# Rows after the experts by plain loads and summed in PSUM, two strict orders, and linear attention's heads by turns

## The chip, the cores and the metric

The kernel runs on one core of a Trainium2 chip. The metric is the device time of one execution in microseconds (us); the times of several runs are given as their median. The engines: PE (TensorE, matrix products) with its weight loads (PEld), DVE (VectorE), ACT (ScalarE), POOL (GpSimd) and SP (SyncE, here a queue that issues transfers). ACT and POOL issue transfers too. Products end in PSUM, everything else is in SBUF or in device memory (DRAM). PE's clock has two levels, 1.2 and 2.4 GHz; the profile gives the granted clock as a share of the higher one.

## The reference

A transformer block of two layers over 512 latent and 256 context rows of 1024 columns, then a second block of another kind over the 512 latent rows. Per layer of the first block, in the reference's words:

```python
h_lat = layer_norm(ALPHA * h_lat + mods[:, :, 2] * o_lat, ln_g[i, 0], ln_b[i, 0])   # after the mixer
f_lat = modulate(h_lat, mods[:, :, 3], mods[:, :, 4])
y_lat = moe(f_lat)                                       # each row goes to two of 32 experts
h_lat = layer_norm(ALPHA * h_lat + mods[:, :, 5] * y_lat, ln_g[i, 1], ln_b[i, 1])
```

Layer 0 does the same for the context rows, and layer 1's mixer begins by modulating the result. The second block begins with a root-mean-square norm, and one of its three branches is a gated linear attention in chunks, four heads with keys of 64 and values of 128.

## The kernel before

The rows live in `self.res`, six blocks of 128 rows by 1024 columns. Each expert scatters its weighted product rows to a DRAM buffer `y_d` by indirect transfers on POOL's queue (`store`, L1632 ff.): the first choices of all rows in its first half, the second choices in its second. Rows that overflow an expert's two halves of 64 go through up to a few extra tiles (`extra`), each of them behind a branch; in this data layer 0 has two extra tiles, of which the second fills both halves, and layer 1 has none.

Two places read `y_d` back. The first is the start of layer 1's mixer (`mixer_cd`), six blocks; the second the start of the second block (`second_body`), four. At both, `products` (L1729) loads the first half on ACT's queue into a buffer and accumulates the second half straight into `self.res` by a transfer of POOL's queue; then an addition on DVE (or, for two blocks at the second place, POOL) makes the sum with the residual, and a layer norm follows: statistics by `bn_stats` in two halves, an inverse root by a chain of one-column DVE operations, and a scale and shift on ACT (`normed`, first place) or on DVE (second place).

First place: each block is then turned by eight PE transposes and modulated (`modulate`), half by ACT, half by DVE; the result is split into a high and a low part (ACT rounds, POOL subtracts, L465) and projected by `project_window`, whose `finish` turns queries and keys one block later. Weights stream through four raw buffers on SP's queue (`Stream`) and are split into high and low parts in the same way, by ACT (L247) and DVE (L248). On POOL, `gain` and `bias` of the norm are applied to the first four blocks of `self.res` (L1069, L1070), whose result is needed only after the attention.

Second place: `front` adds, norms, writes the rows to DRAM, and norms them again; `back` turns and splits them and projects V. `piped(4, front, back, 2)` runs `front` two blocks ahead.

At both places the framework's planner orders the instructions of each engine, from its own costs. Under `tc.manual_schedule(engines=...)` the named engines keep the order in which the code is written; the experts' loop already does that for PE, ACT and DVE.

Linear attention (`gla`): for two pairs of heads and eight levels, each head's four blocks of 128 rows make products of 64 rows by 128 columns (L2091), into a PSUM tile per head; a masked copy on DVE (L2092) takes each tile into `ST`. The two heads of a pair lie in rows 0 to 63 and 64 to 127. The other branch's convolution projections fill in between.

Of the kernel before, what the change touches and what calls it, by code (L numbers as in the profile page):

```python
# [13 lines left out]
F32 = mybir.dt.float32  # L14
# [9 lines left out]
P = 128  # L24
# [159 lines left out]
class Kern:  # L184
# [262 lines left out]
    def modulate(self, x, b, layer, aT, places, ps):  # L447
# [3 lines left out]
        for k0 in (0, 4):  # L451
# [13 lines left out]
            (nc.gpsimd if layer else nc.vector).tensor_sub(aT[1][:, k0:k0 + 4, tok], v, aT[0][:, k0:k0 + 4, tok])  # L465
# [338 lines left out]
    def mixer_cd(self, atp, then):  # L804
# [3 lines left out]
        with ExitStack() as es:  # L808
# [15 lines left out]
            ys, at = [t[:, i * D:(i + 1) * D] for i in range(2)], [t[:, i * 512:(i + 1) * 512] for i in (4, 5, 6)]  # L824
            t = qp.tile([P, 3584], F32, tag="QK", name="t_qk")
            ys, gain = ys + [t[:, i * D:(i + 1) * D] for i in range(2)], t[:, 2 * D:3 * D]
            ys += [qp.tile([P, D], F32, tag=x, name="ys") for x in ("VW", "KX")]
            bias = qp.tile([P, D], F32, tag="VW", name="bias")
# [3 lines left out]
            for b in range(NB):  # L832
                self.products(0, b, ys[b])
# [5 lines left out]
            st = Stream(self, sp, plan, 4, 5, 768)  # L839
            nc.sync.dma_start(gain, self.bcast_rows(A["ln_g"][0, 1], D))  # L840
            nc.sync.dma_start(bias, self.bcast_rows(A["ln_b"][0, 1], D))
# [7 lines left out]
            nc.vector.tensor_scalar_mul(nsink, sink, -1.0)  # L849
# [200 lines left out]
            pc = ps.tile([P, 2, 2, KC], F32, tag="aux", name="pc")  # L1050
            for i in range(2):
                self.transpose(pc[:, i].rearrange("p w k -> p (w k)"), shsc[i])
            nc.scalar.activation(self.mcol[:, 1].rearrange("p i k w -> p i w k"), pc, AF.Copy)
# [1378 lines left out]
```

## Time and profile before

| | |
|---|---|
| time, median of 3 runs | 3341.03 us (3340.9 to 3345.55) |
| profiled execution's own time | 3345.23 us |
| its span | 3343.4 us, mean granted clock 0.958 |
| PE busy | 3016.8 us, 90% |
| DVE busy | 1502.2 us, 45% |
| ACT busy | 1015.6 us, 30% |
| POOL busy | 608.1 us, 18% |
| DMA | 647 MB, mean 194 GB/s |

The span is from the first to the last instruction of the profiled execution; its own time is 1.8 us longer. A matrix product of fp32 operands shows as two records. Busy shares are averages over stages with different limits, so stages are read one by one below.

### The profile page before, as it was taken

How to read it: one execution, taken by the hardware profiler on the slowest of the kernel's cores; microseconds unless marked ns; L12 is line 12 of the kernel's file. 1: busy time of each engine (PE TensorE's matmuls, PEld its weight loads, DVE VectorE, ACT ScalarE, POOL GpSimd, SP SyncE). 2: the span in 40 equal slices, each digit the busy share in tenths (PEclk: the TensorE clock that was granted, in tenths of full speed). 3: DMA queues.
4: the chain of work that ended last, by engine and by line, in shares of the span. 5: the costliest groups of instructions: out<-in, count | busy, mean ns of one | idle time of the engine just before them, and what ended most of it. 6: DMA issues, size and time to landing. Idle time of an engine off the chain costs nothing. (4 is left out here: it accounts for less than half of the span.)

```text
span 3343.4 us, 50272 instructions
## 1 busy us (share of the span) xinstructions
PE 3016.8 (90%) x19017; PEld 2180.2 (65%) x19017; DVE 1502.2 (45%) x3382; ACT 1015.6 (30%) x2180; POOL 608.1 (18%) x572
## 2 busy tenths in 40 slices
PE   7999999799999938998799998579999999979998
PEld 4677757555555527887555544258788777758887
DVE  3578866443222247765521212254544443364533
ACT  2445561111111015764111111123343433233321
POOL 1101012243422233011221211110221400010000
PEclk9999999799999968999799999889899999989999
DMA  7433152999999741113697999822121222322232
GB/s 268 157 98 106 58 170 105 356 393 418 393 419 418 313 143 37 51 42 109 242 386 283 411 418 403 322 97 75 58 79 64 76 73 91 139 78 99 101 120 76
DMA packets 142672, 647.34 MB, mean 194 GB/s; under 512 B 27458, under 2 KB 35170, under 8 KB 81074
## 3 DMA queue, kind: packets, MB, share of 16 engines
q1 hardware_dynamic: 117346, 598.03, 46.3%
q0 software_dynamic: 22192, 36.24, 3.5%
q10 hardware_dynamic: 2848, 9.19, 0.8%
q8 instruction: 187, 3.06, 0.4%
q14 instruction: 99, 0.81, 0.1%
HBM read 670.18 MB, written 35.03 MB: 211 GB/s over the span
## 5 line engine op out<-in xcount | busy, mean ns | idle before, releaser
L1600 PE MATMUL u<-raw,xs 128*64 128x256 f32 x5312 | 596.6, 382 | 19.6 <-DMA raw<-in_k_w 19.3
L1600 PEld LDWEIGHTS u<-raw,xs 128*64 128x64 f32 x5312 | 378.3, 137 | 219.0 <-DMA raw<-in_k_w 23.1
L248 DVE TENSOR_TENSOR wl<-raw,wh 128x2048 fp32r<-128x2048 f32 (+3 forms) x146 | 257.3, 1768 | 392.3 <-ACT wh L247 391.5
L241 PE MATMUL pm<-hTh,wh 128*128 128x512 f32 x872 | 343.7, 394 | 1.7 <-DVE hTl L248 1.4
L243 PE MATMUL pm<-hTh,wl 128*128 128x512 f32 x872 | 341.3, 392 | 1.1 <-DVE wl L248 1.1
L242 PE MATMUL pm<-hTl,wh 128*128 128x512 f32 x872 | 341.7, 392 | 0.0
L247 ACT ACTIVATE wh<-raw 128x2048 fp32r<-128x2048 f32 (+3 forms) x148 | 219.3, 1487 | 390.9 <-PE pm L242 178.0
L1620 PE MATMUL y<-raw,gs 128*64 128x512 f32 x1328 | 300.4, 597 | 4.3 <-ACT gs L1615 1.5
L1605 DVE TENSOR_TENSOR sg<-sg,u 128x256 f32<-128x256 f32 x132 | 55.4, 421 | 513.5 <-PEq L1653 299.8
L243 PE MATMUL pm<-wh,aTl 128*128 128x384 f32 (+2 forms) x576 | 200.8, 349 | 8.4 <-POOL aTl L465 8.4
L241 PE MATMUL pm<-wh,aTh 128*128 128x384 f32 (+2 forms) x576 | 203.3, 354 | 3.7 <-ACT wh L247 2.0
L242 PE MATMUL pm<-wl,aTh 128*128 128x384 f32 (+2 forms) x576 | 199.1, 346 | 0.6 <-DVE wl L248 0.6
L1620 PEld LDWEIGHTS y<-raw,gs 128*64 128x64 f32 x1328 | 89.0, 136 | 169.6 <-issue 155.7
L1604 ACT ACTIVATE sg<-u 128x256 f32<-128x256 f32 x132 | 50.8, 385 | 481.6 <-PE u L1600 315.9
L1626 DVE SCALAR_TENSOR_TENSOR ys<-y,rt_sw,gate 128x512 f32<-128x512 f32 x128 | 93.5, 748 | 226.3 <-PE y L1620 226.3
L241 PEld LDWEIGHTS pm<-hTh,wh 128*128 128x128 f32 x872 | 163.6, 188 | 37.6 <-DVE hTl L248 1.8
L243 PEld LDWEIGHTS pm<-hTh,wl 128*128 128x128 f32 x872 | 163.5, 188 | 36.1 <-DVE wl L248 1.6
L242 PEld LDWEIGHTS pm<-hTl,wh 128*128 128x128 f32 x872 | 163.6, 188 | 34.3
L1615 ACT ACTIVATE gs<-t 128x512 f32<-128x512 f32 x66 | 39.5, 598 | 332.7 <-PE t L271 301.9
L1298 POOL DMA_INDIRECT xg<-f_d,rt_row x64 | 68.5, 1070 | 395.8 <-PE t L271 369.3
L271 PE MATMUL t<-ident,p 128*128 128x128 f32 x704 | 122.0, 284 | 6.7 <-ACT pT L888 1.0
L243 PEld LDWEIGHTS pm<-wh,aTl 128*128 128x128 f32 x576 | 114.4, 199 | 15.0 <-POOL aTl L465 10.0
(559 smaller groups left out, 5551.2 us busy)
## 6 DMA issues: line engine op xcount, KB each, us to landing
raw<-in_k_w SPq DMA_DIRECT2D x408, 1024.0 KB
raw<-in_k_sb SPq DMA_DIRECT2D x79, 1024.0 KB
raw<-in_mod_w SPq DMA_DIRECT2D x160, 256.0 KB
raw<-in_k_ab SPq DMA_DIRECT2D x24, 384.0 KB
raw<-in_k_cd SPq DMA_DIRECT2D x24, 384.0 KB
raw<-in_k_mod SPq DMA_DIRECT2D x8, 1024.0 KB
raw<-in_k_w_out SPq DMA_DIRECT2D x8, 1024.0 KB
raw<-in_k_sb SPq DMA_DIRECT2D x12, 512.0 KB
```

The costliest lines, as they stand in the source:

```text
L241: nc.tensor.matmul(out, lh, rh, start=start, stop=False)
L242: nc.tensor.matmul(out, lh, rl, start=False, stop=False)
L243: nc.tensor.matmul(out, ll, rh, start=False, stop=stop)
L247: self.nc.scalar.activation(h, x, AF.Copy)
L248: (sub or self.nc.vector).tensor_sub(l, x, h)
L271: self.nc.tensor.transpose(out, in_, self.ident[:k, :k])
L1298: self.nc.gpsimd.indirect_dma_start(out=x, out_offset=None, in_=self.f_d[:nb * P], in_offset=bass.IndirectOffsetOnAxis(ap=gi, axis=0), bou ...
L1600: nc.tensor.matmul(pu[c][i][64 * n:64 * n + 64], xs[:, k, tok], w[:, k % 4, n * 256:(n + 1) * 256], start=k == 0, stop=k == KC - 1)
L1604: nc.scalar.activation(sg[c], pu[c][0], AF.Silu)
L1605: nc.vector.tensor_mul(sg[c], sg[c], pu[c][1])
L1620: nc.tensor.matmul(py[c][64 * n:64 * n + 64], gs[:, c, k % 2, k // 2], W[k // 2][:, k % 2, n * 512:(n + 1) * 512], start=k == 0, stop=k == 3)
L1626: nc.vector.scalar_tensor_tensor(y, py[c], sw[:, 0], gate[:, 0], op0=OP.mult, op1=OP.mult)
```

## The change

Four edits. (1) `products` loads both halves by plain transfers, the first on ACT's queue, the second on SP's; nothing is accumulated by a transfer. `summed` adds the residual and both loaded rows in PSUM, by products with the identity: three per half of 512 columns. The norms read PSUM. Blocks 0 and 1 are loaded ahead of the first weights, the others behind. (2) Both starts are written in one strict order for PE, ACT, DVE and POOL. At the second place `front` is now in two parts, one block ahead. At the first place gain and bias are loaded into buffers of the last block and applied after the ordered stretch, and the modulation's subtraction runs on DVE. (3) In an extra tile the second scatter runs only if the second half has rows. (4) In the linear attention the products of the two heads alternate.

```diff
@@ modulate
-            (nc.gpsimd if layer else nc.vector).tensor_sub(aT[1][:, k0:k0 + 4, tok], v, aT[0][:, k0:k0 + 4, tok])
+            nc.vector.tensor_sub(aT[1][:, k0:k0 + 4, tok], v, aT[0][:, k0:k0 + 4, tok])
@@ mixer_cd
-            for b in range(NB):
-                self.products(0, b, ys[b])
+            for b in range(2):
+                self.products(0, b, *ys[b])
+            st = Stream(self, sp, plan, 4, 5, 768)
+            for b in range(2, NB):
+                self.products(0, b, *ys[b])
...
-            Ws = [st.get() for _ in range(4)]
-            first = project_window(0, Ws)
-            for b in range(NB + 1):
-                if b < NB:
-                    x = self.res[:, b]
-                    nc.vector.tensor_add(x, x, ys[b])
-                    self.normed(self.small, x, x, 1e-5 / ALPHA ** 2)
-                if b:
-                    n = self.res[:, b - 1]
-                    self.modulate(n, b - 1, 1, aT, at, ps)
-                if b > 1:
-                    next(first)
-            next(first)
+            def front(b):
+                x = self.res[:, b]
+                self.normed(self.small, self.summed(x, ys[b], ps), x, 1e-5 / ALPHA ** 2)
+            with tc.manual_schedule(engines={E.PE, E.Activation, E.DVE, E.Pool}):
...
+                front(0)
+                Ws = [st.get(0) for _ in range(4)]
+                first = project_window(0, Ws)
+                for b in range(NB + 1):
+                    if 0 < b < NB - 1:
+                        front(b + 1)
+                    if b < NB:
+                        self.modulate(self.res[:, b], b, 1, aT, at, ps)
+                    if b == 0:
+                        front(1)
+                    else:
+                        next(first)
+            gain, bias = last_ys
+            nc.sync.dma_start(gain, self.bcast_rows(A["ln_g"][0, 1], D))
+            nc.sync.dma_start(bias, self.bcast_rows(A["ln_b"][0, 1], D))
@@ experts, extra tiles
-                        for c in range(2):
-                            store(scaled(c, sw[:, c]), si[:, c:c + 1])
+                        ys = [scaled(c, sw[:, c]) for c in range(2)]
+                        store(ys[0], si[:, 0:1])
+                        with tc.If(store_more):
+                            store(ys[1], si[:, 1:2])
@@ products
-        self.nc.scalar.dma_start(out, self.y_d[b * P:(b + 1) * P])
-        self.nc.gpsimd.dma_start(self.res[:, b], self.y_d[(n + b) * P:(n + b + 1) * P], accum_op=OP.add)
+        self.nc.scalar.dma_start(first, self.y_d[b * P:(b + 1) * P])
+        self.nc.sync.dma_start(second, self.y_d[(n + b) * P:(n + b + 1) * P])
+    def summed(self, x, ys, ps):
+        pm = ps.tile([P, 2, 512], F32, tag="s", name="sum")
+        for n in range(2):
+            for i, t in enumerate((x, *ys)):
+                self.nc.tensor.matmul(pm[:, n], self.ident, t[:, n * 512:(n + 1) * 512], start=i == 0, stop=i == 2)
+        return pm.rearrange("p a c -> p (a c)")
@@ second_body
                 for b in range(4):
-                    self.products(1, b, second[b])
+                    self.products(1, b, *ys[b])
+                    if b == 1:
+                        nc.gpsimd.dma_start(g, self.bcast_rows(A["pre_mix_g_2"], D))
+                        self.ws = ws = weights()
...
-                    (nc.gpsimd if b > 1 else nc.vector).tensor_add(x, x, second[b])
-                    mean, r = self.norm_scale(self.small, x, 1e-5 / ALPHA ** 2)
-                    nc.vector.scalar_tensor_tensor(x, x, mean, gb[:, 0], op0=OP.subtract, op1=OP.mult)
+                    y = self.summed(x, ys[b], ps)
+                    mean, r = self.norm_scale(self.small, y, 1e-5 / ALPHA ** 2)
+                    yield
+                    nc.vector.scalar_tensor_tensor(x, y, mean, gb[:, 0], op0=OP.subtract, op1=OP.mult)
                     nc.vector.scalar_tensor_tensor(x, x, r, gb[:, 1], op0=OP.mult, op1=OP.add)
                     nc.sync.dma_start(self.x_d[b * P:(b + 1) * P], x)
-                    return self.rms_apply(x, g, xp)
+                    yield self.rms_apply(x, g, xp)
...
-                for _ in piped(4, front, back, 2):
-                    pass
+                with tc.manual_schedule(engines={E.PE, E.Activation, E.DVE, E.Pool}):
+                    f = front(0)
+                    next(f)
+                    n = next(f)
+                    Ws = [ws.get(0) for _ in range(2)]
+                    for b in range(4):
+                        if b < 3:
+                            f = front(b + 1)
+                            next(f)
+                        back(b, n)
+                        if b < 3:
+                            n = next(f)
+                        values(b)
@@ gla
+                    pg = [ps.tile([P, 512], F32, tag="aux", name="pg") for _ in range(2)]
+                    for b in range(4):
+                        t = slice(b * P, (b + 1) * P)
+                        for hh in range(2):
+                            d = slice(hh * 64, (hh + 1) * 64)
+                            nc.tensor.matmul(pg[hh][:, t], ls[d, t], rs[d, t], start=True, stop=True)
                     for hh in range(2):
-                        d = slice(hh * 64, (hh + 1) * 64)
-                        pg = ps.tile([P, 512], F32, tag="aux", name="pg")
-                        for b in range(4):
-                            t = slice(b * P, (b + 1) * P)
-                            nc.tensor.matmul(pg[:, t], ls[d, t], rs[d, t], start=True, stop=True)
```

## Rows read from the trace of the kernel before

**Rows 1.** Stretches: busy PE, PEld, DVE, ACT, POOL (instructions), clock, DMA share, GB/s

```profile
1194.70:1236.40 41.70, 0.54 (x2) 0.36 (x3) 16.11 (x39) 4.48 (x6) 5.45 (x7) 0.50 0.90 255
...
1236.40:1300.50 64.10, 44.52 (x218) 38.76 (x218) 49.74 (x122) 30.26 (x72) 37.64 (x24) 0.79 0.13 42
...
1300.50:1350.00 49.50, 47.99 (x363) 41.85 (x362) 42.92 (x136) 31.62 (x102) 5.84 (x7) 0.97 0.10 30
...
2147.00:2194.70 47.70, 0.04 (x1) 0.07 (x2) 27.06 (x69) 6.12 (x6) 12.97 (x10) 0.53 0.70 214
...
2194.70:2227.80 33.10, 31.46 (x224) 29.46 (x224) 16.31 (x51) 11.87 (x18) 2.88 (x2) 0.90 0.18 62
...
2290.00:2390.00 100.00, 98.31 (x549) 78.84 (x548) 55.12 (x88) 26.02 (x38) 3.31 (x5) 1.00 0.18 64
```

**Rows 2.** Timeline after the first experts: start, length (us), engine, line, operation

```profile
1194.72 1.78 SPq L66 DMA_DIRECT2D raw<-in_k_cd  x4
...
1196.63 0.84 ACTq L1732 DMA_DIRECT2D t_o<-y_d  x2
...
1235.11 1.24 ACT L445 ACTIVATE res<-res,ln_m,rs_y 128x1024 f32<-128x1024 f32 x1 [25.75 <-DVE ln_m L444]
...
1236.40 1.97 PE L271 MATMUL pt<-ident,res 128*128 128x128 f32 x8 [35.54 <-ACT res L445]
```

**Rows 3.** DMA issues after the first experts: count, size, median us to landing

```profile
res<-y_d POOLq DMA_DIRECT2D x6, 512.0 KB, 30.4
```

**Rows 4.** Lines that copy V: count, ns min/median/max, first, last start

```profile
L914 ACT ACTIVATE V<-pm x12: 203/221/235, 1255.4 to 1361.0; 128x64 f32<-128x64 f32 x12
...
L1816 ACT ACTIVATE V<-pm x4: 574/598/598, 2204.7 to 2227.8; 128x512 f32<-128x512 f32 x4
```

**Rows 5.** Timeline of PE, dilated attention's fp32 score products

```profile
2520.77 1.02 PE L2230 MATMUL s<-qk 128*128 128x512 f32 x2
...
2521.63 0.61 PE L2232 MATMUL s<-qk 128*128 128x128 f32 x4
```

**Rows 6.** Timeline at the second place

```profile
2151.63 1.98 ACTq L1732 DMA_DIRECT2D y<-y_d  x4
...
2193.06 1.28 DVE L1749 SCALAR_TENSOR_TENSOR rm_n<-res,rs_y,g 128x1024 f32<-128x1024 f32 x1
...
2194.66 1.94 PE L271 MATMUL pt<-ident,rm_n 128*128 128x128 f32 x8 [48.37 <-DVE rs_t L262]
...
2258.77 2.29 DVE L248 TENSOR_TENSOR wl<-raw,wh 128x2048 fp32r<-128x2048 f32 x1 [3.27 <-ACT wh L247]
```

**Rows 7.** Timeline of PE while the clock rises

```profile
2200.95 0.40 PE L242 MATMUL pm<-wl,hTh 128*128 128x256 f32 x1
...
2201.31 0.28 PE L241 MATMUL pm<-wh,hTh 128*128 128x256 f32 x1
```

**Rows 8.** Timeline of DVE, first place: one-column operations, one modulation

```profile
1246.05 2.09 DVE L266 SCALAR_TENSOR_TENSOR rs_y<-rs_t,rs_y 128x1 f32<-128x1 f32 x1
...
1248.06 0.40 DVE L461 TENSOR_SCALAR t_o<-pt,mcol 128x128 f32<-128x128 f32 x1
...
1265.45 0.14 DVE L257 TENSOR_SCALAR rs_i<-ln_v 128x1 int32<-128x1 int32 x1
...
1267.23 0.16 DVE L444 SCALAR_TENSOR_TENSOR ln_m<-ln_mv,rs_y 128x1 f32<-128x1 f32 x1
```

**Rows 9.** The subtraction's line on either engine

```profile
L465 DVE TENSOR_TENSOR aTl<-at,aTh x12: 672/688/693, 35.2 to 94.6; 128x512 fp32r<-128x512 f32 x12
...
L465 POOL TENSOR_TENSOR aTl<-t_o,aTh x12: 1262/1277/1511, 1243.3 to 1295.2; 128x512 fp32r<-128x512 f32 x12
```

**Rows 10.** Timeline of PE, linear attention

```profile
2309.95 1.76 PE L2091 MATMUL pg<-Pl 64*128 64x128 f32 x16 [0.27 <-DVE ST L2092]
```

**Rows 11.** Timeline of PE, experts' products on alternate column halves

```profile
1149.75 6.46 PE L1600 MATMUL u<-raw,xs 128*64 128x256 f32 x58
```

**Rows 12.** Timeline of PE's weight loads while routing, clock low

```profile
608.05 1.35 PEld L1366 LDWEIGHTS pp<-tok,marks 128*128 128x128 f32 x6 [2.04 <-DVE marks L1362]
```

More of the change, by code (lines that the diff above doesn't have):

```diff
@@ L823, in mixer_cd @@
             t = op_.tile([P, 7 * NLAT], F32, tag="oT", name="t_o")
[L824 to L828, printed above, removed]
+            last_ys, at = [t[:, i * D:(i + 1) * D] for i in range(2)], [t[:, i * 512:(i + 1) * 512] for i in (4, 5, 6)]
+            qk = [qp.tile([P, 3584], F32, tag="QK", name=f"t_qk{i}") for i in range(2)]
+            qk = [[t[:, i * D:(i + 1) * D] for i in range(3)] for t in qk]
+            vw, kx = ([qp.tile([P, D], F32, tag=x, name="ys") for _ in range(2)] for x in ("VW", "KX"))
+            ys = [*qk[0], *vw, *kx, *qk[1], *last_ys]
+            ys = [ys[2 * b:2 * b + 2] for b in range(NB)]
             shsc = [ap.tile([16, P], F32, tag="v", name="shsc") for _ in range(2)]
@@ L1704, in extra @@
                     for i, (gi, sw, si) in zip(js, tables):
-                        more = nc.values_load(gi[64:65], engines=[E.PE], min_val=0, max_val=2000000) < nt
+                        more, store_more = (nc.values_load(gi[64:65], engines=[eng], min_val=0, max_val=2000000) < nt
+                                            for eng in (E.PE, E.Pool))
                         W = s.take(4)
@@ L1727, in experts, with products @@
             extra(0)
-    def products(self, layer, b, out):
+    def products(self, layer, b, first, second):
         n = 4 if layer else 6
-        self.nc.scalar.dma_start(out, self.y_d[b * P:(b + 1) * P])
-        self.nc.gpsimd.dma_start(self.res[:, b], self.y_d[(n + b) * P:(n + b + 1) * P], accum_op=OP.add)
+        self.nc.scalar.dma_start(first, self.y_d[b * P:(b + 1) * P])
[6 more added lines that the diff above has]
+        return pm.rearrange("p a c -> p (a c)")
     def rms_scale(self, x, pool):
@@ L1779, in proj, with second_body @@
             self.mm3(pm[:, c:c + n], self.hTh[:, k, tok], self.hTl[:, k, tok], w[0][:, k], w[1][:, k], k == 0, k == KC - 1)
-    def second_body(self):
+    def second_body(self, weights):
         nc, tc, A = self.nc, self.tc, self.A
-        ws, proj_T = self.ws, self.proj_T
+        proj_T = self.proj_T
         with ExitStack() as es:
@@ L1793, in second_body @@
                 g = xp.tile([P, D], F32, name="g", bufs=1)
-                nc.gpsimd.dma_start(g, self.bcast_rows(A["pre_mix_g_2"], D))
-                second = [xp.tile([P, D], F32, tag="y", name="y", bufs=4) for _ in range(4)]
+                ys = [[xp.tile([P, D], F32, tag=f"y{b}{i}", name="y", bufs=1) for i in range(2)] for b in range(4)]
                 for b in range(4):
-                    self.products(1, b, second[b])
+                    self.products(1, b, *ys[b])
+                    if b == 1:
+                        nc.gpsimd.dma_start(g, self.bcast_rows(A["pre_mix_g_2"], D))
+                        self.ws = ws = weights()
                 gb = self.res[:, 4:6]
```

22 lines of the change are left out of this document (10 added, 12 removed).

## The prediction

> **What bounds the kernel now.** I read the page first: TensorE (PE) is busy for 90% of the span, and the slices show three dips. Then the table by stretches [rows 1], which says what each dip is. Two of them lie where this change works. After the first experts PE does 0.5 us of work in 41.7 us at a DMA share of 0.90, and then runs at a mean granted clock of 0.79, busy 44.5 of 64.1 us, while VectorE (DVE) is the fuller engine for what it has to do (49.7). After the second experts PE does nothing for 47.7 us and then is busy 31.5 of 33.1. The linear attention (2290 to 2390) is the opposite: PE 98.3 of 100 at full clock, DVE 55. So in the first two places what ends last is a wait for rows of products, and in the third it is PE itself.
>
> The timeline at the first place [rows 2] shows the loads released at 1194.7, when the last scatter of the experts lands, and the first normalised block leaving ScalarE (ACT) at 1235.1; PE's 35.5 us of waiting ends there. Beside the loads run six accumulating transfers of 512 KB which take 30.4 us each from issue to landing [rows 3]. The checkpoint I use for both places is the line that copies V out of PSUM, once per block [rows 4]: at the first place block 0 comes at 1255.4 and block 5 at 1300.5 (9.0 per block), at the second 2204.7 to 2227.8 (7.7 per block).
>
> **What a sum in PSUM costs.** Six fp32 identity products of 512 columns per block: 36 at the first place and 24 at the second. The nearest row is the score product of the dilated attention, of the same shape [rows 5]: a product appears as two records, and the next one starts 0.86 us later at full clock. Six are 5.2 us a block; at the lower level twice that. Coming from a long idle PE stays at the lower level for 6.5 us (first transpose at 2194.66 [rows 6], products 0.40 us long until 2201, 0.28 after [rows 7]). So the first sum after the wait takes 6.5 us for the first 3.25 and 1.95 for the rest, 8.4. This is new work on PE; it removes one 1.2 us addition per block from DVE or GpSimd (POOL), the accumulating traffic, and the waits on it.
>
> **First place, step by step.** (a) The pair of rows for block 0 is now issued first on two queues, ACT's at 1196.6 as before [rows 2]; 1.05 MB at the 255 GB/s of this stretch [rows 1] is 4.1 us, with a little for the small loads ahead of it: landed about 1202. (b) Sum 8.4: 1210.4. (c) Statistics: the second half, 0.64 (half of a 1.28 pass [rows 6]), and the chain of one-column operations, 1.9 from shift to scale [rows 8] plus 0.4 for two before it: 2.9; the pass on ACT 1.24 [rows 2]: 1214.6. (d) Eight transposes at the low level, 1.97 [rows 2]: 1216.6. (e) In the written order the sum of block 1 stands behind these transposes, partly at the low level (7), and that of block 2 (5.3) behind it: PE is at 1229. DVE meanwhile does the four weight splits, block 0's rounding and block 1's statistics. Transposes of block 1, then the projection of block 0 (24 products of 384 columns; at the second place 48 of 256 take 5.9 us, see there, so by columns 0.18 each: 4.4, up to half more with the clock low): V of block 0 at about 1236, 19 us ahead of now.
>
> From there it loses. The cycle in the written order runs across engines: sum 5.4, statistics 2.9, pass 1.24, ACT's part of the modulation 2.1 (four modulations at about 0.38, and a rounding at half a pass), the subtraction 0.69 [rows 9], DVE's four modulations (0.40 each with a little overlap [rows 8]) 1.4, and only then is a PSUM buffer free for the last QK transposes (0.5), behind which the next sum stands: 14.2 us against 9.0 now. PE's own work in it is 12.0, DVE's about 10, so neither engine sets it but the order. Block 1 follows block 0 by 10.7 while the pipe fills, blocks 2 and 3 by 14.2 each, the context blocks, which have no rotation and a narrow projection, by 10.8 and 4: 54 us, so block 5 at 1290, 10.5 us ahead of 1300.5.
>
> (f) The subtraction goes from POOL to DVE, 1.28 to 0.69 each [rows 9]; PE waited for it, and the sum above holds the new price. (g) The eight multiplications and additions of gain and bias, POOL's 2.4 us each, move from this stage to the one after it, as they now wait for rows that the last sum frees. Today they stretch DVE's one-column operations from 0.15 to as much as 2.1 us [rows 8]. In the next stage DVE is busy 42.9 of 49.5 us and PE 48.0 [rows 1]: little is hidden there. The bounds are 0 and 8 times 2; I take 5, nearer the low end, as many operations there read PSUM, and a PSUM read among the stretched ones keeps its 0.40 [rows 8]. (h) SP's queue takes six row loads it didn't have, with the first weights after the second; behind them stand the zero rows and the masks. At 255 GB/s all twelve row loads and the weights (7.9 MB) are in by about 1226, the masks soon after; the first attention scores need them after 1290: 0. POOL's queue loses its six loads, and nothing on it waits for more. First place: 5.5 us gained. Bounds: 16 gained, 5 lost.
>
> **Second place.** Pair issued at 2151.6 [rows 6], 1.05 MB at 214 GB/s [rows 1]: 2157. Sum 8.4: 2165.4. Statistics 2.8, two passes 2.5, a squaring pass on ACT 1.3, the chain 1.9, the pass with the gain 1.28: rows ready at 2175 (2194.3 now). Transposes: 2177. But the written order puts the two weight splits (2.29 each [rows 6]) and block 1's statistics (3.4) ahead of block 0's rounding on DVE: its products start at 2184.3. The first block took 8 us from its start while the clock rose, so V of block 0 at 2192, 12 us ahead of now. Then each block costs products 5.9 (7.7 now [rows 4], less 1.0 for transposes and 0.8 of short waits), the next sum 5.4 behind them, its statistics 2.8 and a rounding 0.66: 14.7 instead of 7.7. Today the additions and norms of later blocks lie ahead, on DVE and POOL, while PE waits. Two cycles of 14.7 and a last step of 9.3, which has no sum: 2231, 3 us later than 2227.8. In each cycle PE idles some 2.6 us at a stretch, and at the first place a busy share of 0.7 went with a clock of 0.79 [rows 1]; I add 1 us per cycle. Second place: 6 us lost. Bounds: 3 gained (the pair lands 3 earlier, order as good as now), 16 lost. The weight loads move behind two pairs of rows; they have until 2171 and land by then at this rate.
>
> **The linear attention.** 128 products (64 rows by 128 columns) take their heads in turn. Now 16 records, 8 products, take 1.76 us from first start to last end [rows 10]: 0.1 us a record, 26 us in all, on an engine without slack. If neighbours of different row halves run at once, half goes: 13. One row speaks for it: the experts' products, which use alternate column halves, take 6.46 us for 58 records of 256 columns, 0.11 each [rows 11], where half of the 0.43 us record above is 0.215. So halves of the array do overlap in columns. One speaks against: products with only 32 columns still take 1.35 us for 6 weight loads at the lower level, 0.22 each, so 0.11 at full clock [rows 12], which is also the record's time here; if loads of the two halves take turns, nothing goes. No row shows two row halves. I take the overlap, and 10 of the 13, as the next level's first products now wait for both mask copies rather than one.
>
> The Trainium skill, TensorE: Matmul & The Clock Gate, section What overlaps and what doesn't, has weight loads overlap running matmuls only where the row groups differ. By that rule the 13 us would go almost whole; without it the term is 0, the second case below. The trace bears the rule out for column halves only; no run here shows it for rows.
>
> **The rest.** In an extra tile the second scatter becomes conditional. Its first extra tile skips it, off the path; the last one, on the path, still stores both halves, and the branch lies in its wait for the first scatter: 0, at most 1.2 lost. It would cost if that wait were shorter.
>
> **The sum.** 5.5 gained, 6 lost, 10 gained: 9.5 gained. The profiled execution took 3345.2 us around a span of 3343.4, 4.2 above the median of 3341.0; from its own time 3335.7, from the median 3331.5.
>
> **Rivals.**
> Forecast, 0.50: as above, 3320 to 3345.
> Weight loads of the two heads take turns, so the linear attention gains nothing: 0.5 lost in all, 3341.5. For it: rows 12. Against it: rows 11. Chance 0.25.
> The clock falls back between sums, the slower end. After each sum PE has a wait; if PE's idle stretches put it at the lower level in each cycle, a sum takes 10.3 and the cycles grow to some 18 to 20 at both places: 9 lost at the first with the POOL term, 16 at the second, 10 gained in the attention: 15 lost, 3356. It decides from a mean clock under 0.7 in the two stretches; the 0.79 of the first stretch is not far off. Chance 0.15.
> The order does better than my cycle: work written after the block fills the gaps (next weights, scores), and the rows land at 1200 and 2155: 16 gained, 2 gained, 11 gained, 3312. For it: PE's own work in a cycle is 12.0 of 14.2. Chance 0.10.
>
> About 0.2%, 6.7 us, is what a measurement of this kernel can tell from no change. Of the forecast, 0.63 lies beyond it on the fast side and 0.34 within it; of the second case 0.18 and 0.62; the third is slower, the fourth faster: faster 0.47, same 0.33, slower 0.20. The range reaches from the fourth case to the third, 3312 to 3356; the likeliest case alone is 3320 to 3345.
>
> **What would show it.** Sums: 12 records per block, 0.43 us apart at full clock. First place: V of block 0 near 1236 and 14 us between the next; if they come 10 apart, my cycle is wrong. Second place: 14.7 between V's, the last near 2231. Attention: spacing of records 0.05 or 0.1. POOL's gain operations after 1290 beside stretched one-column operations. I am most likely wrong in the two cycles, each made of some eight durations, and in how far PE's clock holds.

## The result and the profile after

The changed kernel takes 3368.2 us (median of 4 runs, 3363.85 to 3370.1) against 3340.97 for the kernel before: a ratio of 1.0072, 95% interval 1.006 to 1.0085. It is 0.7% slower; 9.5 us of gain were forecast. Its profiled execution has a span of 3366.0 us.

First the page of after, its span and the busy time of each engine. PE is busy for 58 us more than before while the span grows by 23: the sums are there (60 products, two records each), but busy time alone doesn't say where the end was lost.

```profile
span 3366.0 us, 50501 instructions
...
PE 3074.8 (91%) x19137; PEld 2200.4 (65%) x19137; DVE 1500.6 (45%) x3386; ACT 1015.8 (30%) x2180; POOL 576.0 (17%) x547
```

To see where, I compared the start of each instruction with the start of the same one in the trace of before (same line, tiles and shapes, in order) and took the median shift of a stretch:

| stretch, in the time of before | shift of after, us |
|---|---|
| ahead of the first place, 1150 to 1194 | -1.3 |
| behind it, 1330 to 1345 | +26.4 |
| in the attention's first units, 1400 to 1450 | +28.2 |
| ahead of the second place, 2100 to 2147 | +27.0 |
| behind it, 2240 to 2290 | +31.4 |
| behind the linear attention, 2440 to 2500 | +22.9 |
| end, 3280 to 3340 | +22.6 |

So the first place (to 1450) lost 29.5 us, the second 4.3, and the linear attention gained 8.5. Two of the three terms are near their forecast (6 lost, 10 gained); the first has the other sign. The table by stretches of after answers to [rows 1] (columns as there), in the same order: after the first experts while nothing has been projected; from the first transposes to V of block 5; the second place in two parts; the linear attention.

```profile
1193.40:1214.30 20.90, 8.94 (x14) 3.43 (x14) 3.32 (x14) 1.42 (x3) 0.51 (x1) 0.66 0.93 355
1214.30:1327.30 113.00, 76.17 (x278) 51.65 (x278) 59.06 (x151) 33.87 (x76) 23.86 (x12) 0.71 0.15 51
2174.00:2206.00 32.00, 17.58 (x34) 7.89 (x34) 13.72 (x31) 5.94 (x6) 1.72 (x4) 0.69 0.63 244
2206.00:2259.20 53.20, 42.11 (x238) 34.56 (x238) 30.70 (x87) 12.39 (x18) 2.86 (x2) 0.87 0.23 83
2321.40:2412.90 91.50, 90.48 (x540) 71.21 (x539) 53.89 (x86) 25.57 (x37) 3.66 (x6) 1.00 0.20 70
```

The wait did shrink: 41.7 us of the first row of [rows 1] are 20.9 now, and 47.7 at the second place are 32.0. But the next stretch at the first place, 64.1 us before, is 113 long, and in it no engine is busy for more than 76. Nothing is full and all are late; that points to the order, and the experiments below test it. The copies of V, one per block, which answer to [rows 4], first place and then second (timeline of ACT):

```profile
1239.23 0.20 ACT L915 ACTIVATE V<-pm 128x64 f32<-128x64 f32 x1
1251.13 0.20 ACT L915 ACTIVATE V<-pm 128x64 f32<-128x64 f32 x1
1273.83 0.20 ACT L915 ACTIVATE V<-pm 128x64 f32<-128x64 f32 x1
1304.52 0.21 ACT L915 ACTIVATE V<-pm 128x64 f32<-128x64 f32 x1
1318.24 0.22 ACT L915 ACTIVATE V<-pm 128x64 f32<-128x64 f32 x1 [1.13 <-PE pm L243]
1327.34 0.22 ACT L915 ACTIVATE V<-pm 128x64 f32<-128x64 f32 x1 [0.44 <-PE pm L243]
...
2217.47 0.60 ACT L1839 ACTIVATE V<-pm 128x512 f32<-128x512 f32 x1 [2.93 <-PE pm L243]
2234.11 0.60 ACT L1839 ACTIVATE V<-pm 128x512 f32<-128x512 f32 x1 [3.02 <-PE pm L243]
...
2259.22 0.58 ACT L1839 ACTIVATE V<-pm 128x512 f32<-128x512 f32 x1
```

Block 0 is 16 us earlier than before (19 were forecast); then the steps are 11.9, 22.7, 30.7, 13.7 and 9.1, where 14.2 was forecast for a full step. One whole step of 22.7 us, from one block's sum to the next one's, read from the timelines of PE, DVE and ACT:

```profile
1256.54 1.92 PE L1753 MATMUL sum<-res,ident 128*128 128x512 f32 x2
1261.42 1.02 PE L1753 MATMUL sum<-res,ident 128*128 128x512 f32 x2
1264.20 1.29 DVE L430 BATCH_NORM_STATS2 ln_st<-sum 128x6 f32<-128x512 f32 x2 [6.81 <-PE sum L1753]
1268.00 1.21 ACT L445 ACTIVATE res<-sum,ln_m,rs_y 128x1024 f32<-128x1024 f32 x1 [10.94 <-DVE ln_m L444]
1269.10 1.50 ACT L463 ACTIVATE t_o<-pt,mcol 128x128 f32<-128x128 f32 x4
1271.29 0.69 DVE L465 TENSOR_TENSOR aTl<-t_o,aTh 128x512 fp32r<-128x512 f32 x1 [3.39 <-ACT aTh L464]
1271.90 1.36 DVE L461 TENSOR_SCALAR t_o<-pt,mcol 128x128 f32<-128x128 f32 x4
1273.96 0.69 DVE L465 TENSOR_TENSOR aTl<-t_o,aTh 128x512 fp32r<-128x512 f32 x1 [0.69 <-ACT aTh L464]
1274.57 0.48 DVE L531 TENSOR_TENSOR t<-pm,rope 128x320 f32<-128x320 f32 x1
1276.07 0.29 DVE L520 SCALAR_TENSOR_TENSOR QK<-t,QK 64x128 fp32r<-64x128 f32 x1
1276.42 0.47 PE L271 MATMUL t<-ident,qk 128*128 128x128 f32 x1 [5.38 <-DVE QK L520]
1277.59 0.69 PE L271 MATMUL t<-ident,qk 128*128 128x128 f32 x2 [0.70 <-DVE QK L520]
1279.24 1.92 PE L1753 MATMUL sum<-res,ident 128*128 128x512 f32 x2
```

Read it as a ring. Sum of block b+1: 7.7 us. Its statistics, both halves behind the whole sum, and inverse root: 3.8. Its pass on ACT: 1.1. The modulation of block b, written behind that though it doesn't need it: 2.2 on ACT, 2.0 on DVE, then the second half's rounding 0.7 and subtraction 0.6. The rotation of block b-1, behind that on DVE: 1.5. The turns of block b-2's queries, behind that: 3.2, one PE transpose, one ACT copy and one DVE subtraction after another, 1.17 each. And behind the last transpose on PE stands the next sum. All of it together is 22.7 (the steps are rounded); no two of these steps run side by side. The longest waits of PE name the last link (total, times, longest), between 1239 and 1327 in after and between 1255 and 1300 in before:

```profile
PE t L271 <- DVE QK L520: 24.6, 12, 7.6
...
PE t L271 <- DVE QK L520: 3.6, 3, 2.3
```

The step of 30.7 holds something more. From 1290.55 POOL applies gain and bias, 2.4 us a pass, and the inverse root of block 5, whose sum has just ended, falls under it (timelines of POOL and DVE):

```profile
1290.55 4.67 POOL L1079 TENSOR_TENSOR res<-res,t_o 128x1024 f32<-128x1024 f32 x2 [13.79 <-DMA t_o<-in_ln_g]
...
1290.39 0.16 DVE L266 SCALAR_TENSOR_TENSOR rs_y<-rs_t,rs_y 128x1 f32<-128x1 f32 x1
1290.59 2.35 DVE L262 SCALAR_TENSOR_TENSOR rs_t<-rs_y,rs_m 128x1 f32<-128x1 f32 x1
1292.97 2.26 DVE L266 SCALAR_TENSOR_TENSOR rs_y<-rs_t,rs_y 128x1 f32<-128x1 f32 x1
1295.27 2.26 DVE L444 SCALAR_TENSOR_TENSOR ln_m<-ln_mv,rs_y 128x1 f32<-128x1 f32 x1
```

These passes are written after the ordered stretch. The planner put them into the middle of it all the same, as soon as their loads had landed; what the order binds is only what is written inside.

### The profile page after: what moved, and what is told of

Its sections match the earlier page's. It is cut to its first block, busy times and chain, and to the rows that moved or that the text cites. A ratio compares the mean times of both kernels' runs of the same rounds, so it can differ in the third digit from the quotient of the medians.

```text
span 3366.0 us, 50501 instructions
## 1 busy us (share of the span) xinstructions
PE 3074.8 (91%) x19137; PEld 2200.4 (65%) x19137; DVE 1500.6 (45%) x3386; ACT 1015.8 (30%) x2180; POOL 576.0 (17%) x547
## 5 line engine op out<-in xcount | busy, mean ns | idle before, releaser
L1610 PE MATMUL u<-raw,xs 128*64 128x256 f32 x5312 | 597.9, 382 | 19.6 <-DMA raw<-in_k_w 19.2
L1644 POOL DMA_INDIRECT y_d<-ys,rt_si x80 | 80.2, 1003 | 235.3 <-DVE ys L1636 120.1
```

What stands on the lines that cost most here:

```text
L1610: nc.tensor.matmul(pu[c][i][64 * n:64 * n + 64], xs[:, k, tok], w[:, k % 4, n * 256:(n + 1) * 256], start=k == 0, stop=k == KC - 1)
L1644: nc.gpsimd.indirect_dma_start(out=y_rows, out_offset=bass.IndirectOffsetOnAxis(ap=si, axis=0), in_=y, in_offset=None, bounds_check=4 * nt ...
```

## The experiments

My theory after the result: the strict order of the first place is the loss, because it makes every block go through all engines one after another. The rival: the sums on PE are the loss, 36 products of 0.86 us, 31 us. All runs in one table; the last three columns are shifts worked out as above (ahead of the first place to 1450; across the second place; across the linear attention). Unchanged stages move by up to 3 us between kernels, and the last column by 5 (the paragraph on e9 says why), so a difference of that size says nothing. The shifts are those of one profiled execution, which can be some us off the median (e7's took 3304.8 us, its median is 3312.8).

| kernel | median us | ratio to before, 95% | first | second | attention |
|---|---|---|---|---|---|
| the change | 3368.2 | 1.006 to 1.0085 | +29.5 | +4.3 | -8.5 |
| e1_heads_only | 3335.69 | 0.9966 to 0.9989 | +3.0 | -0.5 | -9.2 |
| e2_first_free | 3332.34 | 0.9948 to 0.9976 | -6.0 | +6.1 | -7.8 |
| e3_first_adds_strict | 3357.48 | 1.0024 to 1.0049 | +16.4 | +5.9 | -7.9 |
| e4_first_turned | 3353.14 | 1.0018 to 1.0047 | +13.5 | +5.5 | -7.8 |
| e5_no_gain | 3359.45 | 1.0036 to 1.0069 | +19.6 | +3.8 | -8.5 |
| e6_both_free | 3318.12 | 0.9914 to 0.9947 | -7.6 | -6.5 | -8.6 |
| e7_adds_free | 3312.76 | 0.9897 to 0.993 | -14.6 | -9.2 | -10.2 |
| e8_adds_free_gain_late | 3314.8 | 0.9898 to 0.9931 | -12.5 | -9.2 | -5.0 |
| e9_heads_strict | 3311.25 | 0.9889 to 0.9922 | -14.0 | -9.4 | -9.6 |
| e10_gain_after | 3310.99 | 0.9886 to 0.9919 | -12.7 | -8.5 | -8.0 |
| e11_first_pe_strict | 3355.82 | 1.002 to 1.0048 | +15.6 | +4.1 | -8.5 |
| e12_first_others_strict | 3345.59 | 0.9994 to 1.0015 | +5.8 | +4.5 | -8.6 |
| e13_strict_gain_dve | 3363.39 | 1.0043 to 1.0077 | +24.5 | +3.8 | -8.5 |
| e14_adds_gain_dve | 3304.92 | 0.9871 to 0.9904 | -23.5 | -9.2 | -9.9 |

**Order or sums: e2_first_free, e3_first_adds_strict, e4_first_turned.** e2 takes the order off the first place and leaves all else, the sums too:

```diff
-            with tc.manual_schedule(engines={E.PE, E.Activation, E.DVE, E.Pool}):
-                pc = ps.tile(...)
+            pc = ps.tile(...)
```

> The changed kernel with the strict order taken off the first place: same loads, same sums in PSUM, same loop, but the planner orders the engines. Theory (the order is the loss: one block's cycle goes through every engine once and takes 22.7 us): most of the 29.5 us lost at the first place comes back, with blocks 10 to 13 us apart, in all 3340 to 3346. Rival (the sums on TensorE are the loss, 36 fp32 products of 0.86 us, 31 us): it stays within 6 us of the changed kernel, 3362 to 3368.

e3 keeps the order and makes the sum on DVE:

```diff
-                self.normed(self.small, self.summed(x, ys[b], ps), x, 1e-5 / ALPHA ** 2)
+                for y in ys[b]:
+                    nc.vector.tensor_add(x, x, y)
+                self.normed(self.small, x, x, 1e-5 / ALPHA ** 2)
```

> The changed kernel with the first place's sums made by two additions per block on VectorE (2.4 us) instead of six identity products (5.2 us at full clock, 7.5 as measured in the cycle), strict order kept. Theory (the order is the loss): the cycle only loses the difference, 22.7 to about 18, four cycles, so 3345 to 3355, still slower than before. Rival (the sums are the loss): blocks come 9 us apart again and the whole is at 3335 to 3340.

e4 keeps order and sums and writes the loop's three steps the other way round:

```diff
-                    if 0 < b < NB - 1:
-                        front(b + 1)
-                    if b < NB:
-                        self.modulate(self.res[:, b], b, 1, aT, at, ps)
-                    if b == 0:
-                        front(1)
-                    else:
-                        next(first)
+                    if b:
+                        next(first)
+                    if b < NB:
+                        self.modulate(self.res[:, b], b, 1, aT, at, ps)
+                    if b < NB - 1:
+                        front(b + 1)
```

> The changed kernel with the three steps of the first place's loop written in the opposite order: projection of block b-1, modulation of block b, then sum and norm of block b+1. Strict order kept. Theory (the order is the loss, since the modulation of block b was written behind the statistics of block b+1 on VectorE and ScalarE though it does not need them): the cycle falls from 22.7 to about 15.5 us, four cycles, 25 to 29 us back, 3340 to 3346. Rival (the sums or the clock are the loss): 3362 to 3368.

e2 ends it: the order alone is worth 35.5 us at the first place (+29.5 to -6.0), and with the sums still on PE the blocks come 10 to 11.5 us apart until gain and bias arrive. The copies of V of e2 (timeline of ACT):

```profile
1233.16 0.22 ACT L915 ACTIVATE V<-pm 128x64 f32<-128x64 f32 x1 [0.74 <-PE pm L243]
1243.35 0.22 ACT L915 ACTIVATE V<-pm 128x64 f32<-128x64 f32 x1 [0.67 <-PE pm L243]
1254.75 0.22 ACT L915 ACTIVATE V<-pm 128x64 f32<-128x64 f32 x1 [0.67 <-PE pm L243]
1266.16 0.22 ACT L915 ACTIVATE V<-pm 128x64 f32<-128x64 f32 x1 [1.55 <-PE pm L243]
1285.02 0.22 ACT L915 ACTIVATE V<-pm 128x64 f32<-128x64 f32 x1 [0.20 <-PE pm L243]
```

The step of 11.4 is PE's own work in a step (sum 5.2, transposes 0.9, projection 4.4, turns 0.6: 11.1): PE is busy for 11.0 of it at a granted clock of 1.00, so here PE is the bound, not the order. It came out better than I expected. e3 shows what the sums cost inside the ring: the full step falls from 22.7 to 18.3, about the difference between 7.7 us and two additions. Its total is 2.5 us above the theory's range. Both have a price, but without the sums the order still loses 16.4 us, and without the order the sums lose nothing against before (against additions they cost some 7 us, see e7). e4 gets back 16 of the 25 to 29 us that I expected: its full steps are 18.1 and 17.4, not 15.5, and PE still waits for the turns (9.3 us between 1239 and 1275).

**Which side of the ring: e11_first_pe_strict, e12_first_others_strict.** The order kept on PE alone, and on all but PE:

```diff
-            with tc.manual_schedule(engines={E.PE, E.Activation, E.DVE, E.Pool}):
+            with tc.manual_schedule(engines={E.PE}):
```

```diff
-            with tc.manual_schedule(engines={E.PE, E.Activation, E.DVE, E.Pool}):
+            with tc.manual_schedule(engines={E.Activation, E.DVE, E.Pool}):
```

> The changed kernel with the strict order of the first place on TensorE alone. Theory (the cycle is a ring through all engines, and either side's order alone leaves only that side's work: on TensorE sum 5.3, transposes 0.9, projection 4.4, four turns of queries and keys 4.7): 15 us a block instead of 22.7, 25 us back, 3340 to 3348. Rival (TensorE's order alone carries the loss, as the next sum stands behind the last turn of queries): 3360 to 3368.

> The changed kernel with the strict order of the first place on ScalarE, VectorE and GpSimd, TensorE left to the planner. Theory (a ring): VectorE's side alone has statistics 3.6, pass 1.2, modulation 4.9, rotation 1.5 and the turns 4, 15 us a block if the sum runs ahead, 3340 to 3348. Rival (the order of VectorE and ScalarE alone carries the loss): 3360 to 3368.

The full steps are 17.7 and 17.4 us with PE alone bound, 18.7 and 20.2 with the others alone: either side's order alone still costs, and freeing either side gives back 14 to 24 of the 35.5 us. e11 lies between theory and rival. Its step can be read on PE: turns 4.9, sum 7.7, transposes and projection 5.1. I was short by some 2.5 us a step there: the sum behind the turns again takes 7.7 us, not 5.3, since PE comes to it from their waits. e12's total is where the theory put it, but its steps aren't the theory's 15 us, so that agreement is luck. Passes of gain and bias run in both steps (from 1264.5 on; beside them L465 takes 2.77 us for 0.69), and how much of the steps is the order I didn't separate.

**Gain and bias: e5_no_gain, e8, e10_gain_after, e13_strict_gain_dve.** e5 drops the four multiplications and four additions:

```diff
-            for b in range(4):
-                n = self.res[:, b]
-                nc.gpsimd.tensor_mul(n, n, gain)
-                nc.gpsimd.tensor_add(n, n, bias)
```

> The changed kernel, strict order kept, without the eight multiplications and additions of gain and bias on GpSimd after the first place; they are left out, so the rows that the second experts' norm sees are not the reference's. Theory (while GpSimd runs, VectorE's one-column operations take 2.3 us instead of 0.2; in the changed kernel the eight fall into the cycle of block 4's norm, whose step is 30.7 us where the one before is 22.7): 8 us back, 3359 to 3362. Rival (they are covered, and the 30.7 has another cause): 3366 to 3369.

The step of 30.7, from block 2 to block 3, falls to 23.2 (the expectations call it the fourth, and put block 4's norm into it; it is the third, and holds block 5's), the first column by 9.9 and the whole by 8.8 us (3359.45). In the strict order, then, some 7 to 10 of the 29.5 us are gain and bias. e13 makes the same passes on DVE (`nc.vector` for `nc.gpsimd` in these lines):

> The changed kernel with the eight passes of gain and bias on VectorE (1.2 us each) instead of GpSimd (2.4 us each), strict order kept. Theory (the price is VectorE's stretched one-column operations while GpSimd runs): the stretch is gone, the fourth step of V falls from 30.7 to about 24, VectorE has idle time in the strict cycle for 9.6 us of passes, 3360 to 3363. Rival (the passes themselves are in the way): 3366 to 3371.

That gains 5 of the 8: the one-column operations keep 0.15 to 0.22 us, but the planner sets the eight passes of 1.2 us between them, so this step is 28.3. e8 and e10 (on the version e7 below) asked whether the price can be moved away. e8 only wrote the passes after the first unit of the attention:

> As the one before, with gain and bias loaded into two other buffers and applied on GpSimd only after the first unit of the attention. Theory (their price is what they stretch on VectorE while VectorE is on the path): 5 to 9 us less than the one before. Rival (the price moves along with them into the attention, where VectorE is busy too): within 3 us of it.

It didn't do what it says: the planner issued the first pass at 1235.9, earlier than without the edit, since other buffers were free sooner. So it tells nothing on that question. e10 ties the passes to that unit's output:

```diff
+                if not u:
+                    nc.gpsimd.tensor_copy(gain[:, 0:1], oT[:, 1, NLAT - 1:NLAT])
+                    nc.gpsimd.tensor_copy(bias[:, 0:1], oT[:, 1, NLAT - 1:NLAT])
+                    nc.sync.dma_start(gain, self.bcast_rows(A["ln_g"][0, 1], D))
+                    nc.sync.dma_start(bias, self.bcast_rows(A["ln_b"][0, 1], D))
```

> The version with plain loads and additions on VectorE, with gain and bias applied on GpSimd only after the first unit of the attention, this time tied to it: their loads wait for a copy of that unit's last output (the kernel before this one only wrote them later, and the planner moved them back to 1236). Theory (they cost what they stretch on VectorE while its one-column operations are on the path; in the first place one step of V is 23.5 us where its neighbours take 6 to 10): 6 to 10 us back at the first place, at most 3 of it lost in the attention, 3304 to 3309. Rival (price moves along): 3311 to 3315.

The rival holds. Behind the first place (1330 to 1345) the shift is -26.6, 9 us better than e7's -17.8; by 1400 it is -13.6. The softmax of the attention has one-column sums on DVE as well, and they and the scalings behind them are held in the same way (timeline of DVE, while POOL's passes run from 1339.59):

```profile
1340.38 1.61 DVE L875 TENSOR_TENSOR den<-den 128x1 f32<-128x1 f32 x1 [0.96 <-ACT den L874]
...
1342.22 2.33 DVE L878 TENSOR_SCALAR p<-p,r 128x512 f32<-128x512 f32 x1
```

Until POOL is done, four sums (L875) take 1.1 to 2.3 us instead of 0.16 and four scalings (L878) 1.8 to 2.35 instead of 0.49, 13.4 us more in all, which accounts for the 13 us by which the shift falls back.

**The linear attention: e1_heads_only, e9_heads_strict.** e1 is the kernel before with the last hunk of the change alone.

> The kernel before with only the linear attention's two heads by turns. Theory (row halves overlap): in the trace of the change, products of neighbouring heads start 6 to 7 ns apart, and the stage from 2290 to 2440 ends 8.5 us earlier; alone it should give 8 to 9 us, 3332.5. Rival (the products do not run any faster; the stage only gained because earlier waits moved): 0 to 3 us, 3338 to 3341.

3335.69, 7 us under the kernel before (3342.75 beside it) and so between theory and rival, and 9.2 us in that stage: the gain belongs to the turns and needs nothing else. e9 fixes PE's order inside a level (`manual_schedule` with `E.PE` around the eight products), on e7:

> The version with plain loads and additions on VectorE (3312.8), with TensorE's order of the linear attention's products fixed as written, so that the heads really take turns. In the trace of the change only half of the levels run in pairs (16 records starting over 0.89 us), the others are drawn out over 1.49 us because the second PSUM tile is still being copied. Theory (pairs are worth having): 6 levels times 0.6 us and two last levels of 0.9, 4 to 5 us back, 3308. Rival (TensorE then waits for the copy of the second tile, 0.7 us a level, which the planner's order filled): 0 to 3 us slower, 3313 to 3316.

Two levels in after, one in pairs and one drawn out, and then the first three groups of e9 (timelines of PE):

```profile
2329.21 1.16 PE L2127 MATMUL pg<-Pl 64*128 64x128 f32 x16
...
2331.26 1.76 PE L2127 MATMUL pg<-Pl 64*128 64x128 f32 x16
```

```profile
2272.29 1.16 PE L2129 MATMUL pg<-Pl 64*128 64x128 f32 x16
2274.34 0.48 PE L2129 MATMUL pg<-Pl 64*128 64x128 f32 x2
2275.42 1.16 PE L2129 MATMUL pg<-Pl 64*128 64x128 f32 x14
```

With the order kept, every second level still has its first product alone (2 records, then 14). The levels' time on PE falls from 21.8 to 18.5 us (summed over the groups), yet the column hardly differs (-9.6, e7 -10.2). It adds up two things. From the first level to the last (median shifts of 2270 to 2295 and of 2382 to 2390, in the time of before) the shift falls by 7.0 us in the change and, within 0.4, in every other run with heads by turns; in e9 it falls by 9.2. So the kept order is worth 2.2 us in the levels, about half of the theory's 4 to 5. Part of the 3.3 us saved on the products goes to more changes between kinds of product: there are 24 groups instead of 18, and the first wide product behind a group takes 0.34 us to the next start instead of 0.23. Behind the last level the kernels differ for another reason: over the next 50 us the granted clock is 0.80 in before, 0.83 in the change and in e9, 0.87 in e7 and 0.74 in e8, and the shift changes by -1.4, -0.3, -3.1 and +2.1 in these four runs. That is why e8's column says -5.0, and why e9's 2.2 us don't show in its own.

**Better versions: e6_both_free, e7_adds_free, e14_adds_gain_dve.** e6 takes the order off the second place too. e7 then replaces the sums at both places by two additions on DVE, with `front` two blocks ahead at the second place as before; e14 puts gain and bias on DVE in that version.

> The strict order taken off both places; sums in PSUM kept. With the first place alone freed the whole takes 3332.3, and the second place still loses 5.5 to 6.0 us against before, V 16.6 us apart. Theory (order again): the planner lets products of one block run beside the norm of the next, V about 12.5 us apart, which is TensorE's own work of 5.9 + 5.2 + 1.0; 8 to 10 us back, 3322 to 3325. Rival (at the second place the sums on TensorE are the cost): under 3 us, 3329 to 3333.

> Plain loads kept, sums by two additions per block on VectorE, no strict order at either place, the second place's norms two blocks ahead as before, heads by turns kept. Theory (what the change gains at both places is the earlier start by plain loads, 15 to 20 us each; the order and the sums give it back): V of the first block as early as in the changed kernel, 1239 and about 2178, blocks 9 to 10 us apart, so 12 us gained at the first place, 12 at the second, 8.5 in the linear attention: 3305 to 3312. Rival (VectorE becomes the bound, 2.4 us more per block): blocks 12 us apart, 3318 to 3326.

> The version with plain loads and additions on VectorE, planner's order (3312.8), with the eight passes on VectorE. Theory (stretch): the step of 23.5 us at block 4 falls to 10 to 14, of which VectorE's own 9.6 us give some back, 3303 to 3309. Rival (the passes themselves are in the way): 3311 to 3316.

e6 beats its theory: V at the second place comes 7.7 us apart, not 12.5, because the planner makes all four sums while PE would be waiting (they are done at 2171, the first transposes come at 2174.8):

```profile
2186.25 0.60 ACT L1838 ACTIVATE V<-pm 128x512 f32<-128x512 f32 x1 [7.71 <-PE pm L243]
2193.91 0.60 ACT L1838 ACTIVATE V<-pm 128x512 f32<-128x512 f32 x1 [5.05 <-PE pm L243]
```

So the order costs 12.6 us there as well (+6.1 to -6.5), and the same change without the two orders is 0.7% faster than before instead of 0.7% slower. e7 lies between its theory and its rival at 3312.8; its stages say 7 us more at the first place than e6. Its step at block 4 was still 23.5 us, and e14 brings that to 14.8; e10, with no pass of gain and bias at this place at all, has 15.0 (copies of V, e14 and then e10):

```profile
1250.71 0.22 ACT L915 ACTIVATE V<-pm 128x64 f32<-128x64 f32 x1
1265.51 0.23 ACT L915 ACTIVATE V<-pm 128x64 f32<-128x64 f32 x1
...
1253.05 0.22 ACT L915 ACTIVATE V<-pm 128x64 f32<-128x64 f32 x1
1268.05 0.21 ACT L915 ACTIVATE V<-pm 128x64 f32<-128x64 f32 x1
```

e14 is the best here, 3304.92 us, 1.1% under the kernel before: plain loads, additions and gain on DVE, heads by turns, and no order written out. Its interval still overlaps those of e7, e9 and e10; that it is the best rests on the first column, 9 to 11 us ahead of theirs. The step at block 4 is still twice the 7 us of those ahead of it. The passes aren't the reason, since e10 has the same step without them; made on DVE they cost at most some 2 us at this place (ahead of it to 1345, e14 gains 23.5 and e10 25.7). What fills it I didn't trace further (in e10 DVE is busy for 12.6 of its 14.9 us).

## Why the prediction was wrong, point by point

**The views and the bounds of before** held: the waits at both places ended earlier (20.9 us for 41.7, 32.0 for 47.7), and PE bound the linear attention. That the plain loads alone did the former is likely but not shown; no run changes them by themselves.

**The step that failed is (e), the cycle of the first place.** It was put at 14.2 us "across engines"; it is 22.7. The terms that were there were nearly right, except the sum: 7.7 for 5.4, since PE comes to it from a wait and runs its first products at the lower level (the one of 1256.54 takes 1.71 us to the next start, one at full clock 0.86; in e2, without those waits, a sum takes 5.2), and the statistics: 3.8 for 2.9, since their first half doesn't begin beside the sum but behind it. Missing were steps that the written order puts on the same ring: the second half's rounding and subtraction, 1.3; the rotation of the block before, 1.5; and of the turns I counted the last, 0.5, where all four hand over one after another, 3.2. Sum 2.3, statistics 0.9, and 5.5 of missing steps, with 0.1 less for the pass, are the 8.5. I took the missing ones as running beside; in a strict order nothing does unless it is written there. V of block 5 was due at 1290 and came at 1328.6 (1327.3 and the shift of 1.3): 4.5 of that were there at block 0, 1.2 at block 1, 17 are the two full steps, 8 gain and bias, 2.9 and 5.1 the two context blocks, whose steps still hold the turns of blocks 2 and 3. The bound on the loss, 5 us at the first place, was wrong for the same reason: the bound of a strict order is the sum of all steps of its ring, and that could be added up from the diff and the rows.

**(g), gain and bias,** had the right mechanism and the wrong place. They do wait for buffers that the last sum frees, as I said; but that sum, block 5's, stands in the order three copies of V ahead of the end of the stretch, so they ran inside it, on block 5's inverse root, and cost 7 to 10 us (e5) where I had 5 behind it. Bounds of 0 to 16 held that. That they begin at 1290.55, after the 1290 that I named, is luck: the stretch ended 37 us later than forecast.

**(a) to (d) and (f)** held: rows at 1202.8 (1202 forecast), first V at 1239.2 (1236); its products were done at 1234, and the copy stood behind the modulation on ACT. (h), the queue of SP, showed nothing. Nor did the conditional scatter: ahead of the first place the change is at -1.3 us, and the runs that share this edit lie between -3.1 and +2.8.

**The second place:** 4.3 lost (6 forecast). V of block 0 at 2217.5 less a shift of 27.0 is 2190.5 (2192), steps 16.6, 16.6 and 8.5 (14.7, 14.7, 9.3). Here I had followed the ring through the engines, and it came out, but for the statistics, which again begin behind the whole sum (3.4 for 2.8). The 1 us a cycle for the clock didn't show: the sums at 2217.3 and 2233.9 take 5.2 us. e6 shows what I hadn't weighed: that this order was 12.6 us worse than the planner's with the same sums.

**The linear attention:** 8.5 gained (10). Neighbouring products of the two heads start 6 to 7 ns apart, 16 records over 0.89 us where a head alone takes 0.88 for 8. The row halves do run at once. The rule of the Trainium skill that was weighed for it (TensorE: Matmul & The Clock Gate, What overlaps and what doesn't) agrees with that, as far as starts show. But in each pair of heads only 4 of 8 levels run fully in pairs: summed over its groups the products' time fell from 27.5 to 21.5 us, 6 and not 13. To the last level 7.0 us were gained, in every run with heads by turns but e9 much the same; the other 1.5 came behind it, where the clock differs from run to run. So the forecast of 10 was near by luck, with a smaller part from where I had put it.

I had also misread the trace of before: "No row shows two row halves" is wrong. In 10 of the 16 levels the planner had already mixed the two heads, and 24 of the 256 records start 4 to 6 ns behind another. Merged rows hide the starts but not the length; [rows 10] is such a level, and here are another one, both heads, and one head alone (timeline of PE, before):

```profile
2297.88 1.71 PE L2091 MATMUL pg<-Pl 64*128 64x128 f32 x16
2299.91 1.16 PE L2091 MATMUL pg<-Pl 64*128 64x128 f32 x8 [0.32 <-DVE ST L2092]
```

Sixteen records one behind another, 0.11 us apart, would have taken some 2.05 us. So the overlap could have been read beforehand, and the kernel before already had a part of it: 76 of 256 records start that close in the change, 112 in e9.

**The rivals.** The second, weight loads by turns, is out by e1. The third had the right sign and the wrong mechanism. Its condition, a mean clock under 0.7, was nearly met at the first place (0.71; 0.87 at the second), but of the 8.5 us that a step is longer the clock is mainly the 2.3 in the sum, and its 18 to 20 us a cycle and 3356 fell short. The fourth, "the order does better than my cycle", is what the planner does without the order (e2, 3332; e6, 3318), not what the kernel did. That the predicted 3331.5 is close to e2's 3332.3 is chance in one respect: the first place gives 6.0 there as forecast, but with blocks 11.4 apart rather than 14.2.

## What to carry to other kernels

Before a strict order is written or believed, add up one turn of its loop along all engines, each step behind what is written ahead of it: here 22.7 us, where no engine was busy for more than 14.5. A stretch in which no engine is full and the next block's first step waits for the last block's last step is bound by order. Giving the first place back to the planner was worth 35.5 us here; writing the independent steps first gave 16.0 (e4) and making the dearest step cheaper 13.1 (e3). Work that is written later isn't late by that: it runs when its inputs are there, unless a dependency holds it.

## What the runs showed of the hardware

A one-column DVE operation with two tensor operands in SBUF is held to the end of a POOL pass. In the trace of after L262 takes 0.22 us and, once POOL's passes run, 2.35; wider ones are held too (L465 1.80 for 0.69, L922 1.65 for 0.49); operations with one operand (L257, 0.14) and those that read PSUM (L461) keep their time even then, as the timeline of DVE in e7 shows beside POOL's passes of 1257.75 to 1264.6:

```profile
1257.12 0.14 DVE L257 TENSOR_SCALAR rs_i<-ln_v 128x1 int32<-128x1 int32 x1
1257.62 0.40 DVE L461 TENSOR_SCALAR t_o<-pt,mcol 128x128 f32<-128x128 f32 x1
1257.94 2.17 DVE L262 SCALAR_TENSOR_TENSOR rs_t<-rs_y,rs_m 128x1 f32<-128x1 f32 x1
```

The Trainium skill, SBUF — State Buffer, section Who interferes with whom, has the same rule: a DVE instruction with two SBUF inputs contends with a GpSimd instruction that reads SBUF; one with at most one SBUF input does not, unless it runs in a faster mode that takes both ports. The traces agree, with some 2.2 us for each held operation, and they add the price for a kernel: eight passes of 2.4 us cost 7 to 10 us at the first place and 13 in the attention, and 9 less when DVE makes them itself (first column, e14 against e7). L878 in e10, a scaling of 512 columns from SBUF to SBUF, was held as well; the section names `tensor_scalar` among those that can take both ports in such a mode. No run here shows in which mode it ran.
